# Layer 1's down projection in four parts of seven block products each

## The chip, the core and the metric

The kernel runs on one core of a Trainium2 chip. The metric is the device time of one execution in microseconds (us); smaller is better. Five engines run their own queues of instructions in order: TensorE (PE, with weight loads listed apart as PEld), VectorE (DVE), ScalarE (ACT), GpSimd (POOL) and SyncE (SP). Here SP issues the loads of the weights from HBM, and POOL issues transfers that add one buffer onto another on their way. An instruction waits for others by semaphores.

## What is computed

A trunk of two layers on 512 tokens of width 1024, all in float32. Each layer has a mixer and then a gated feed-forward network (FFN) of width 2816, both with a residual. The part that matters is the FFN:

```python
def gated_conv_ffn(x, w_gate, w_up, conv_w, conv_b, w_down):
    g = jnp.einsum('bsd,df->bsf', x, w_gate)
    g = causal_dwconv3(g, conv_w) + conv_b
    up = jnp.einsum('bsd,df->bsf', x, w_up)
    return jnp.einsum('bsf,fd->bsd', jax.nn.silu(g) * up, w_down)
```

After layer 1 follow the residual, `h = h + gated_conv_ffn(...)`, and a final RMSNorm.

## The kernel before

**Numbers in two parts.** The matmuls run in a format (F32R) shorter than float32. Each operand is therefore split: `hi` is the value rounded by an ACT copy, `lo` is the rest, by a DVE subtraction. A product is three matmuls: hi hi, hi lo, lo hi (`mm3`, L132). Weights come through `fetch` (L108: a load on SP's queue into a buffer with tag `raw`, of which there are 4, 512 KB each) and then `parts` (L125: ACT copy, DVE subtraction) or `summed` (L114). `summed` makes `lo` without DVE: ACT writes the negative of the rounded value (L120), POOL issues a transfer that adds the raw value onto it (L121), and ACT copies the `hi` (L122). Split weights lie in buffers with tags `whi` and `wlo`, 6 each.

**The FFN in tiles.** The 2816 hidden columns are 22 tiles of 128. They are made in pairs by `hidden(f)`. Pairs 0 and 2 are plain (`direct`). Pairs 4, 6, 10, 14 and 18 go through `both`, pairs 8, 12, 16 and 20 through `seven`: these form the gate and up projections (`seven`: the up projection only) as seven products of half blocks in place of eight, a scheme in which sums of weight blocks and of input blocks are multiplied and the products added up in the end. Their matmuls have 256 columns, 12 to a product. The names `s12`, `s34`, `s23`, `s14`, `a11` are such weight blocks; `kept` holds up results, `rows` is the padded gate tile for the convolution. Then `conv` (L502: an ACT copy and two DVE steps at L507), `silu` (L511, ACT), the product of gate and up (DVE), and `act` (L516), which splits the 128 x 512 result into `a_hi` and `a_lo`.

**The down projection of layer 1** is interleaved with that. `PARTS` says which pairs are made before which range of tiles is projected:

```python
PARTS = (((0, 2), 0, 2), ((4,), 2, 6), ((6, 8), 6, 10), ((10, 12), 10, 14),
         ((14, 16), 14, 18), ((18, 20), 18, 22))
```

In `ffn1` (L957) each part fetches its down weights one tile at a time (128 rows x 1024, `dn`), and `group8` (L1038) runs 8 PSUM banks: 4 blocks of 128 tokens by 2 halves of 512 output columns. For each bank it goes over the part's tiles, with the activations as the stationary operand and 512 columns of weights as the moving one: 3 matmuls for each tile and bank, 96 for four tiles. When a bank is complete, DVE adds it onto `y` (L1010), which began as the transposed residual. In the last part (tiles 18 to 21) the final norm follows.

**Order.** The kernel's text gives the dependencies, and a scheduler fixes ahead of time the order of instructions on each engine and the buffer that each tile gets. In that order the first matmuls of a part's down projection are those of its two older tiles, for several banks, and those of the two younger ones come in later. PSUM has 7 banks for matmul results and one for other uses.

Of the kernel before, what the change touches and what calls it, by code (L numbers as in the profile page):

```python
# [30 lines left out]
def tile_trunk(ctx: ExitStack, tc: tile.TileContext, x, norm_mix, norm_ffn, final_norm,  # L31
# [3 lines left out]
    nc = tc.nc  # L35
    x = x[0]
# [4 lines left out]
    tp = ctx.enter_context(tc.tile_pool(name="tp", bufs=2))  # L41
# [3 lines left out]
    def mm_bank(name):  # L45
        return ps_mm.tile([P, 512], F32, tag="mm", name=name)
# [61 lines left out]
    def fetch(src, a, b, name):  # L108
        raw = wp.tile([P, a, b], F32, tag="raw", bufs=4, name=f"raw_{name}")
        nc.sync.dma_start(raw, src)  # L110
        return raw, a, b, name

    def weights(src, a, b, name):
        return parts(*fetch(src, a, b, name))  # L114

    def summed(raw, a, b, name):

        hi = wp.tile([P, a, b], F32R, tag="whi", bufs=6, name=f"whi_{name}")
        lo = wp.tile([P, a, b], F32R, tag="wlo", bufs=6, name=f"wlo_{name}")
        nc.scalar.activation(lo, raw, AF.Copy, scale=-1.0)  # L120
        nc.gpsimd.dma_start(lo, raw, accum_op=ALU.add)  # L121
        nc.scalar.activation(hi, raw, AF.Copy)  # L122
        return hi, lo

    def parts(raw, a, b, name):  # L125
        hi = wp.tile([P, a, b], F32R, tag="whi", bufs=6, name=f"whi_{name}")
        lo = wp.tile([P, a, b], F32R, tag="wlo", bufs=6, name=f"wlo_{name}")
        nc.scalar.activation(hi, raw, AF.Copy)  # L128
        nc.vector.tensor_tensor(lo, raw, hi.bitcast(F32), ALU.subtract)  # L129
        return hi, lo  # L130
# [113 lines left out]
    def split(pool, src, name, scale=1.0, tag="a", bufs=None):  # L244
        hi = pool.tile([P, S], F32R, tag=f"{tag}hi", bufs=bufs, name=f"{name}_hi")
        lo = pool.tile([P, S], F32R, tag=f"{tag}lo", bufs=bufs, name=f"{name}_lo")
        nc.scalar.activation(hi, src, AF.Copy, scale=scale)  # L247
        if isinstance(scale, float):
            nc.vector.tensor_tensor(lo, src, hi.bitcast(F32), ALU.subtract)  # L249
        else:  # L250
            nc.vector.scalar_tensor_tensor(lo, src, scale, hi.bitcast(F32),
                                           op0=ALU.mult, op1=ALU.subtract)
        return hi, lo
# [223 lines left out]
    HALF = S // 2  # L477
# [10 lines left out]
    class Ffn:  # L488
# [5 lines left out]

        def __init__(self, layer, prm, norm, ap, sums):
            self.layer, self.prm, self.ap, self.acts = layer, prm, ap, {}
            self.norm, self.sums = norm, sums
            self.t23, self.t41 = {}, {}  # L500

        def conv(self, t, ft):  # L502
            ap, prm, n = self.ap, self.prm, f"{self.layer}_{ft}"
            c = ap.tile([P, S], F32, tag="c", bufs=2, name=f"c{n}")
            nc.scalar.activation(c, t[:, 0:S], AF.Copy, scale=prm("cf", ft))
            for i in (1, 2):
                nc.vector.scalar_tensor_tensor(c, t[:, i : S + i], prm("cf", i * NF + ft), c,  # L507
                                               op0=ALU.mult, op1=ALU.add)
            return c

        def silu(self, c, ft):  # L511
            s = self.ap.tile([P, S], F32, tag="s", bufs=3, name=f"s{self.layer}_{ft}")
            nc.scalar.activation(s, c, AF.Silu, bias=self.prm("bf", ft))  # L513
            return s

        def act(self, ft, s):  # L516
            self.acts[ft] = split(self.ap, s, f"a{self.layer}_{ft}", tag="a", bufs=4)

        def pair_weights(self, f, order, by_dma=""):

# [439 lines left out]
    def ffn1(norm):  # L960
        with tc.tile_pool(name="f1", bufs=1) as ap:
            def sums(kp):
                return [cp.tile([P, 2, HALF], F32R, tag=f"h{k}", name=f"t23_{k}")
                        for k in (kp, kp + NP)]

            ffn = Ffn(1, prm1, norm, ap, sums)
            acts = ffn.acts
            y = [ap.tile([P, D], F32, name=f"y{t}") for t in range(NT)]
            ssf = ap.tile([P, NT, PAD], F32, name="ssf")[:, :, :2]

            def turn_residual(t, half):
                ps = mm_bank(f"hT{t}_{half}")
                for i in range(4):
                    nc.tensor.transpose(ps[:, i * P : (i + 1) * P],
                                        h[half * 4 + i][:, t * P : (t + 1) * P], ident)
                nc.scalar.copy(y[t][:, half * 512 : (half + 1) * 512], ps)

            def before(i, j):
                if i < 2:
                    turn_residual(j, i)  # L980

            for groups, a, b in PARTS:
                for f in groups:
                    ffn.hidden(f, before=before)
                last = b == NF
                if last:
                    fin = wp.tile([P, D], F32, tag="raw", bufs=4, name="fin")
                    nc.scalar.dma_start(
                        fin, final_norm.rearrange("(o d) -> o d", o=1).to_broadcast([P, D]))
                    root = small[:, 2:3]  # L990
                    nc.scalar.activation(root, eps, AF.Sqrt)
                ch = {}
                for ft in range(a, b):
                    ch[ft] = weights(w_ffn_down[1][ft * P : (ft + 1) * P, :]
                                     .rearrange("(k p) c -> p k c", p=P), 1, D, f"dn1_{ft}")

                def lhs(ft, j):
                    ts_ = slice((j // 2) * P, (j // 2 + 1) * P)
                    return acts[ft][0][:, ts_], acts[ft][1][:, ts_]

                def rhs(ft, j):
                    c = slice((j % 2) * 512, (j % 2 + 1) * 512)
                    return ch[ft][0][:, 0, c], ch[ft][1][:, 0, c]

                yf = {}

                def done(j, ps):
                    t, half = j // 2, j % 2
                    dst = y[t][:, half * 512 : (half + 1) * 512]
                    nc.vector.tensor_tensor(dst, ps, dst, ALU.add)  # L1010
                    if not last:
                        return
                    sq = tp.tile([P, S], F32, tag="sq", name=f"sqf{j}")
                    ss = ssf[:, t, half : half + 1]
                    nc.scalar.activation(sq, dst, AF.Square, accum_out=ss)
                    yf[half] = ap.tile([P, S], F32, tag="s", bufs=3, name=f"yf{j}")
                    nc.vector.tensor_tensor(yf[half], dst, fin[:, half * 512 : (half + 1) * 512],
                                            ALU.mult)
                    if half == 0:
                        nc.vector.tensor_scalar(ss, ss, 1.0 / D, EPS, op0=ALU.mult, op1=ALU.add)  # L1020
                        return
                    ms = ssf[:, t, 0:1]
                    nc.vector.scalar_tensor_tensor(ms, ss, 1.0 / D, ms, op0=ALU.mult, op1=ALU.add)
                    r = tp.tile([P, LINE], F32, tag="rc", name=f"rc_fin{t}")[:, :1]
                    newton(ms, 1, f"fin{t}", r)
                    nc.vector.tensor_scalar(ms, ms, 1.5, None, op0=ALU.add)
                    for c in range(2):
                        cs = slice(c * 512, (c + 1) * 512)
# [18 lines left out]
    n = mixer0()  # L1047
    n = ffn0(n)
    n = mixer1(n)
    ffn1(n)  # L1050


# [28 lines left out]
```

## Time and profile before

| | us |
|---|---|
| median of 3 runs | 1006.06 |
| fastest, slowest run | 1005.46, 1007.25 |
| span of the profiled execution | 1004.4 |

The profile is of one execution. Its span reaches from its first to its last instruction; no other time is listed for that execution. Times inside it are counted from the span's start. Layer 1's FFN is the last third, about 640 to 1004 us. A row of a timeline gives the start, the duration, the engine, the line and operation, what is written and what is read, and in brackets the idle time before it and what ended it. A row of the stage table gives, for a stretch, the busy time of each engine with the number of instructions. The chain of waits follows the work that ended last back through what released it.

### The profile page before, as it was taken

What the parts mean: (1) busy time and instruction counts of PE and PEld (TensorE: products, weight loads), DVE (VectorE), ACT (ScalarE), POOL (GpSimd) and SP (SyncE); (2) the same over time, 40 slices, a digit from 0 to 9 for tenths busy, and PEclk for the clock granted to TensorE, in tenths of its full rate; (3) what the DMA queues carried; (4) which work ended last, traced back from release to release, by engine and by line L of the source; (5) the groups of instructions that cost most, each with busy time, mean ns of one, the idle gap of its engine ahead of it and who ended that gap; (6) DMA issues with size and microseconds to landing.
All of it is one profiled execution on the core that took longest, in us unless ns stands there. A gap on an engine that the chain in (4) does not pass through costs nothing.

```text
span 1004.4 us, 14019 instructions
## 1 busy us (share of the span) xinstructions
PE 992.1 (99%) x5547; PEld 865.9 (86%) x5547; DVE 666.0 (66%) x993; ACT 499.9 (50%) x735; POOL 94.1 (9%) x109
## 2 busy tenths in 40 slices
PE   8999999999999999999999999999999999999997
PEld 6888888898989989899878888888989898898985
DVE  5977457968584775847833645389675857658567
ACT  6523345754553635537645434675535365353553
POOL 3032030200000000000300001212000000000000
PEclk9999999999999999999999999999999999999999
DMA  7532234554445444454433123435545345353432
GB/s 236 178 105 84 85 90 122 117 155 114 118 142 131 128 110 119 138 137 127 127 125 104 63 85 105 101 88 123 150 100 153 105 127 147 94 152 112 127 85 84
DMA packets 80749, 120.30 MB, mean 120 GB/s; under 512 B 4164, under 2 KB 53548, under 8 KB 80684
## 3 DMA queue, kind: packets, MB, share of 16 engines
q1 hardware_dynamic: 73580, 98.96, 30.9%
q0 software_dynamic: 5760, 18.88, 10.7%
q10 hardware_dynamic: 1344, 1.58, 0.5%
q8 instruction: 43, 0.70, 0.3%
q14 instruction: 22, 0.18, 0.1%
HBM read 98.42 MB, written 2.10 MB: 100 GB/s over the span
## 4 chain that ended last, share of the span: by engine, by line
PE 95%; DMA 2%; DVE 2%; ACT 1%; SPq 0%; issue 0%; POOL 0%; DVEq 0%; ACTq 0%; POOLq 0%
PE dn L133 4%; PE dn L135 4%; PE dn L134 4%; PE d L133 4%; PE d L134 4%; PE d L135 4%; PE gu L133 3%; PE g L133 3%; PE g L134 3%; PE gu L134 3%; PE gu L135 3%; PE g L135 3%; PE u L135 1%; PE oo L133 1%; PE oo L135 1%; PE u L134 1%
## 5 line engine op out<-in xcount | busy, mean ns | idle before, releaser
L507 DVE SCALAR_TENSOR_TENSOR c<-rows,prm,c 128x512 f32<-128x512 f32 x88 | 68.9, 792 | 0.3
L134 PE MATMUL d<-a_lo,whi_d 128*128 128x512 f32 x176 | 68.6, 390 | 0.0
L135 PE MATMUL d<-a_hi,wlo_d 128*128 128x512 f32 x176 | 68.5, 389 | 0.0
L133 PE MATMUL dn<-whi_dn,a_hi 128*128 128x512 f32 x176 | 68.4, 390 | 0.0
L134 PE MATMUL dn<-wlo_dn,a_hi 128*128 128x512 f32 x176 | 68.4, 390 | 0.0
L135 PE MATMUL dn<-whi_dn,a_lo 128*128 128x512 f32 x176 | 67.6, 390 | 0.0
L133 PE MATMUL d<-a_hi,whi_d 128*128 128x512 f32 x176 | 67.1, 390 | 0.0
L1010 DVE TENSOR_TENSOR y<-dn,y 128x512 f32<-128x512 f32 x48 | 32.3, 688 | 30.9 <-PE dn L135 30.7
L133 PE MATMUL g<-hgh,whi_g 128*128 128x512 f32 x128 | 50.0, 391 | 0.0
L134 PE MATMUL g<-hgl,whi_g 128*128 128x512 f32 x128 | 50.0, 391 | 0.0
L135 PE MATMUL g<-hgh,wlo_g 128*128 128x512 f32 x128 | 49.8, 389 | 0.0
L129 DVE TENSOR_TENSOR wlo_dn<-raw_dn,whi_dn 128x1024 fp32r<-128x1024 f32 x22 | 26.8, 1222 | 30.7 <-ACT whi_dn L128 30.7
L129 DVE TENSOR_TENSOR wlo_d<-raw_d,whi_d 128x1024 fp32r<-128x1024 f32 x22 | 26.8, 1221 | 30.2 <-ACT whi_d L128 30.2
L129 DVE TENSOR_TENSOR wlo_u<-raw_u,whi_u 128x1024 fp32r<-128x1024 f32 x16 | 19.6, 1223 | 34.2 <-ACT whi_u L128 34.1
L120 ACT ACTIVATE wlo_g<-raw_g 128x1024 fp32r<-128x1024 f32 x14 | 14.7, 1050 | 51.6 <-PE dn L134 51.6
L292 DVE TENSOR_TENSOR h<-d,h 128x512 f32<-128x512 f32 x48 | 32.4, 686 | 11.6 <-PE d L135 11.1
L513 ACT ACTIVATE s<-c,prm 128x512 f32<-128x512 f32 x44 | 31.6, 718 | 16.7 <-DVE c L507 16.6
L135 PEld LDWEIGHTS dn<-whi_dn,a_lo 128*128 128x128 f32 x176 | 33.0, 188 | 7.4 <-DVE a_lo L249 0.2
L134 PEld LDWEIGHTS d<-a_lo,whi_d 128*128 128x128 f32 x176 | 33.1, 188 | 7.1 <-DVE a_lo L249 0.2
L133 PEld LDWEIGHTS dn<-whi_dn,a_hi 128*128 128x128 f32 x176 | 33.1, 188 | 7.0 <-ACT a_hi L247 0.2
L133 PEld LDWEIGHTS d<-a_hi,whi_d 128*128 128x128 f32 x176 | 32.9, 188 | 7.0
L135 PEld LDWEIGHTS d<-a_hi,wlo_d 128*128 128x128 f32 x176 | 33.0, 188 | 6.8
(972 smaller groups left out, 3196.0 us busy)
## 6 DMA issues: line engine op xcount, KB each, us to landing
raw_g<-in_w_ffn_gate_dram SPq DMA_DIRECT2D x36, 512.0 KB, 4.5
raw_u<-in_w_ffn_up_dram SPq DMA_DIRECT2D x36, 512.0 KB, 3.8
raw_d<-in_w_ffn_down_dram SPq DMA_DIRECT2D x22, 512.0 KB, 3.6
raw_dn<-in_w_ffn_down_dram SPq DMA_DIRECT2D x22, 512.0 KB, 4.4
wlo_u<-raw_u POOLq DMA_DIRECT2D x18, 512.0 KB, 5.2
wlo_g<-raw_g POOLq DMA_DIRECT2D x14, 512.0 KB, 4.5
raw_oe<-in_w_out_even_dram SPq DMA_DIRECT2D x8, 512.0 KB, 3.5
raw_g<-in_w_ffn_gate_dram SPq DMA_DIRECT2D x16, 256.0 KB, 2.9
```

The costliest lines, as they stand in the source:

```text
L120: nc.scalar.activation(lo, raw, AF.Copy, scale=-1.0)
L129: nc.vector.tensor_tensor(lo, raw, hi.bitcast(F32), ALU.subtract)
L133: nc.tensor.matmul(ps, lhs[0], rhs[0], start=start, stop=False)
L134: nc.tensor.matmul(ps, lhs[0], rhs[1], start=False, stop=False)
L135: nc.tensor.matmul(ps, lhs[1], rhs[0], start=False, stop=stop)
L292: nc.vector.tensor_tensor(h[k], ps, h[k], ALU.add)
L507: nc.vector.scalar_tensor_tensor(c, t[:, i : S + i], prm("cf", i * NF + ft), c, op0=ALU.mult, op1=ALU.add)
L513: nc.scalar.activation(s, c, AF.Silu, bias=self.prm("bf", ft))
L1010: nc.vector.tensor_tensor(dst, ps, dst, ALU.add)
```

## The change

For the four parts with tiles 2 to 17, the down projection of four tiles is done by a new function, `down(a)`. It takes the activations as a 2 x 2 block matrix (two halves of 256 tokens by two pairs of tiles) and the weights as one (two pairs of tiles by two halves of 512 output columns), and forms seven products of sums of blocks. A product has 2 token blocks x 2 tiles x 3 matmuls of 512 columns, 84 for the seven. Their results share three pairs of banks: products 1, 6, 7 and 4 add up in pair `a`, 5 and 3 in pair `e`, and 2 has pair `b`. After each product the pair's current content is added onto `y`, so the next product onto the same pair has to wait for that addition, and there are 14 additions for 8.

The weights of a part come as four blocks of 256 rows x 512 columns (`b11`, `b21`, `b12`, `b22`). Four weight sums (t1 to t4) are formed by DVE, three of them in place in the raw buffers, and all four are split by `summed`; b11, b21 and b22 by `parts`. The activations of tiles 2 to 17 are not split by `act` any more. The rows of two tiles stay in one float32 buffer (`rows`), and `down` forms four sums and splits seven blocks of 128 x 2 x 256. To make room, the convolution's tile `c` takes buffers that other temporaries share, and the pair of `silu` rows is one tile in both layers.

The core of the diff:

```diff
         def conv(self, t, ft):
-            c = ap.tile([P, S], F32, tag="c", bufs=2, name=f"c{n}")
+            c = tp.tile([P, S], F32, tag="sq", name=f"c{n}")
...
         def silu(self, c, ft):
-            s = self.ap.tile([P, S], F32, tag="s", bufs=3, name=f"s{self.layer}_{ft}")
+            f = ft - ft % 2
+            if f not in self.rows:
+                self.rows[f] = self.ap.tile([P, 2, S], F32, tag="s", bufs=3,
+                                            name=f"s{self.layer}_{f}")
+            s = self.rows[f][:, ft % 2, :]
...
         def act(self, ft, s):
-            self.acts[ft] = split(self.ap, s, f"a{self.layer}_{ft}", tag="a", bufs=4)
+            if ft not in self.kept:
+                self.acts[ft] = split(self.ap, s, f"a{self.layer}_{ft}", tag="a",
+                                      bufs=4 if self.layer == 0 else 3)
...
-            ffn = Ffn(1, prm1, norm, ap, sums)
+            ffn = Ffn(1, prm1, norm, ap, sums, range(2, 18))
...
+            def down(a):
+                g1, g2 = ffn.rows[a], ffn.rows[a + 2]
+                name = f"dn{a}"
+
+                def part(src, n, by_dma=False):
+                    hi = ap.tile([P, 2, HALF], F32R, tag="ahi", bufs=3, name=f"hi{n}_{a}")
+                    lo = ap.tile([P, 2, HALF], F32R, tag="alo", bufs=3, name=f"lo{n}_{a}")
+                    nc.scalar.activation(hi, src, AF.Copy)
+                    nc.vector.tensor_tensor(lo, src, hi.bitcast(F32), ALU.subtract)
+                    return hi, lo
...
+                a11, a21 = g1[:, :, :HALF], g1[:, :, HALF:]
+                a12, a22 = g2[:, :, :HALF], g2[:, :, HALF:]
+                b11, b21, b12, b22 = block(0, 0), block(1, 0), block(0, 1), block(1, 1)
+                mov, stat = {}, {}
+                mov[1] = parts(*b11)
+                stat[1] = part(a11, 1)
+                mov[2] = parts(*b21)
+                t1, t4, t3 = b11[0], b21[0], b12[0]
+                minus(t1, b12[0], b11[0])
+                t2 = ap.tile([P, 2, 512], F32, tag="sum", bufs=3, name=f"t2_{a}")
+                minus(t2, b22[0], t1)
+                mov[6] = summed(t2, 2, 512, f"{name}_t2")
+                mov[5] = summed(t1, 2, 512, f"{name}_t1")
+                minus(t3, b22[0], b12[0])
+                mov[7] = summed(t3, 2, 512, f"{name}_t3")
+                minus(t4, b21[0], t2)
+                mov[3] = parts(*b22)
+                mov[4] = summed(t4, 2, 512, f"{name}_t4")
+
+                s1, s2 = (tp.tile([P, 2, HALF], F32, tag="rstd", name=f"as{i}_{a}")
+                          for i in range(2))
+                nc.vector.tensor_tensor(s1, a21, a22, ALU.add)
+                stat[2] = part(a12, 2)
+                minus(s2, s1, a11)
+                stat[6] = part(s2, 6)
+                stat[5] = part(s1, 5)
+                minus(s1, a11, a21)
+                stat[7] = part(s1, 7)
+                minus(s2, a12, s2)
+                stat[3] = part(s2, 3)
+                stat[4] = part(a22, 4)
+
+                chain = {1: "a", 2: "b", 6: "a", 5: "e", 7: "a", 3: "e", 4: "a"}
+                onto = {1: (0, 0), 2: (0, 0), 6: (0, 1), 5: (1, 1), 7: (1, 1), 3: (0, 1),
+                        4: (1, 0)}
+                banks = {}
+                for product in (1, 2, 6, 5, 7, 3, 4):
+                    (hi, lo), (whi, wlo) = stat[product], mov[product]
+                    half, c = onto[product]
+                    for i in range(2):
...
+                        for k in range(2):
+                            for l, r, end in ((hi, whi, False), (hi, wlo, False),
+                                              (lo, whi, k == 1)):
+                                nc.tensor.matmul(ps, l[:, k, ts_], r[:, k, :], start=first,
+                                                 stop=end, skip_group_check=True)
+                                first = False
+                        dst = y[2 * half + i][:, c * 512 : (c + 1) * 512]
+                        nc.vector.tensor_tensor(dst, ps, dst, ALU.add)
...
+                if a in (2, 6, 10, 14):
+                    down(a)
+                    continue
```

Here `block(r, c)` fetches the rows of tile pair `r` and the columns of half `c`, `minus(dst, x, y)` is a DVE subtraction, and `mm_bank` gives a PSUM bank. In the text below hi2 and lo2 are the two parts of the activation block of product 2, and so on.

More of the change, by code (lines that the diff above doesn't have):

```diff
@@ L488, in tile_trunk, with __init__ @@
     class Ffn:
-        def __init__(self, layer, prm, norm, ap, sums):
+        def __init__(self, layer, prm, norm, ap, sums, kept=()):
             self.layer, self.prm, self.ap, self.acts = layer, prm, ap, {}
@@ L500, in __init__ @@
             self.t23, self.t41 = {}, {}
+            self.rows, self.kept = {}, kept
         def conv(self, t, ft):
             ap, prm, n = self.ap, self.prm, f"{self.layer}_{ft}"
-            c = ap.tile([P, S], F32, tag="c", bufs=2, name=f"c{n}")
+            c = tp.tile([P, S], F32, tag="sq", name=f"c{n}")
             nc.scalar.activation(c, t[:, 0:S], AF.Copy, scale=prm("cf", ft))
@@ L964, in sums @@
                         for k in (kp, kp + NP)]
-            ffn = Ffn(1, prm1, norm, ap, sums)
+            ffn = Ffn(1, prm1, norm, ap, sums, range(2, 18))
             acts = ffn.acts
-            y = [ap.tile([P, D], F32, name=f"y{t}") for t in range(NT)]
+            y_all = ap.tile([P, NT, D], F32, name="y")
+            y = [y_all[:, t, :] for t in range(NT)]
             ssf = ap.tile([P, NT, PAD], F32, name="ssf")[:, :, :2]
@@ L980, in before, with block, minus @@
                     turn_residual(j, i)
+            def down(a):
[7 more added lines that the diff above has]
+                    return hi, lo
+                def block(r, c):
+                    rows = slice((a + 2 * r) * P, (a + 2 * r + 2) * P)
+                    return fetch(w_ffn_down[1][rows, c * 512 : (c + 1) * 512]
+                                 .rearrange("(k p) c -> p k c", p=P), 2, 512, f"{name}_{r}{c}")
+                def minus(dst, x, y_):
+                    nc.vector.tensor_tensor(dst, x, y_, ALU.subtract)
+                a11, a21 = g1[:, :, :HALF], g1[:, :, HALF:]
[36 more added lines that the diff above has]
+                    for i in range(2):
+                        at = chain[product], i
+                        first = at not in banks
+                        if first:
+                            banks[at] = mm_bank(f"{name}{at[0]}{i}")
+                        ps = banks[at]
+                        ts_ = slice(i * P, (i + 1) * P)
+                        for k in range(2):
[6 more added lines that the diff above has]
+                        nc.vector.tensor_tensor(dst, ps, dst, ALU.add)
@@ L1015, in done @@
                     nc.scalar.activation(sq, dst, AF.Square, accum_out=ss)
-                    yf[half] = ap.tile([P, S], F32, tag="s", bufs=3, name=f"yf{j}")
+                    if half == 0:
+                        yf["pair"] = ap.tile([P, 2, S], F32, tag="s", bufs=3, name=f"yf{j}")
+                    yf[half] = yf["pair"][:, half, :]
                     nc.vector.tensor_tensor(yf[half], dst, fin[:, half * 512 : (half + 1) * 512],
```

## The prediction

> **What bounds the kernel now.** I read the page first (span, busy time, the shares of the chain that ended last), then the busy time by stage, then the timelines of the engines around one down projection of layer 1.
>
> ```profile
> span 1004.4 us, 14019 instructions
> PE 992.1 (99%) x5547; PEld 865.9 (86%) x5547; DVE 666.0 (66%) x993; ACT 499.9 (50%) x735; POOL 94.1 (9%) x109
> ...
> PE 95%; DMA 2%; DVE 2%; ACT 1%; SPq 0%; issue 0%; POOL 0%; DVEq 0%; ACTq 0%; POOLq 0%
> ```
>
> TensorE carries 95% of the chain. One part of the layer (here tiles 6 to 9) has three stages; the columns are length, then busy time of PE, PEld, DVE, ACT and POOL, clock, DMA share, GB/s.
>
> ```profile
> 744.40:764.70 20.30, 20.30 (x170) 20.18 (x170) 13.42 (x19) 12.35 (x19) 0.86 (x1) 1.00 0.58 156
> 764.70:785.70 21.00, 21.00 (x134) 19.09 (x133) 14.52 (x22) 13.86 (x22) 0.85 (x1) 1.00 0.55 151
> 785.70:807.50 21.80, 21.80 (x99) 17.98 (x98) 14.12 (x23) 4.53 (x6) 0.85 (x1) 1.00 0.26 73
> ```
>
> First row: hidden tiles 6 and 7 (`both`), second: 8 and 9 (`seven`), third: the down projection. TensorE never pauses; the others have room on average. How fast it goes is read from starts, since busy times overlap (48 down matmuls, then the first of the next stage):
>
> ```profile
> 691.37 0.39 PE L133 MATMUL dn<-whi_dn,a_hi 128*128 128x512 f32 x1
> ...
> 702.03 0.39 PE L135 MATMUL dn<-whi_dn,a_lo 128*128 128x512 f32 x1
> 702.25 0.28 PE L624 MATMUL g_4a<-hgh,whi_a 128*128 128x256 f32 x1
> 702.37 0.28 PE L624 MATMUL g_4a<-hgl,whi_a 128*128 128x256 f32 x1
> ```
>
> (702.25 - 691.37)/48 = 0.2267 us for each 512-column matmul, and 0.12 for a 256-column one; the 0.39 is a latency.
>
> **What the change removes.** A part has 4 tiles x 8 banks x 3 = 96 matmuls; the seven products have 12 each, 84. So 12 x 0.2267 = **2.72 us less per part, 10.9 in four**: the down stage would last 19.04 instead of 21.8.
>
> **What it adds.** Durations as steps between back-to-back starts:
>
> ```profile
> 745.15 1.23 DVE L634 TENSOR_TENSOR wlo_s34g<-s34g,whi_s34g 128x1024 fp32r<-128x1024 f32 x1
> 746.30 1.22 DVE L634 TENSOR_TENSOR wlo_s12u<-s12u,whi_s12u 128x1024 fp32r<-128x1024 f32 x1
> 747.43 0.69 DVE L730 TENSOR_TENSOR s<-raw_u,raw_u 128x512 f32<-128x512 f32 x1
> 748.03 0.69 DVE L732 TENSOR_TENSOR s<-raw_u 128x512 f32<-128x512 f32 x1
> ...
> 783.09 0.75 DVE L507 SCALAR_TENSOR_TENSOR c<-rows,prm,c 128x512 f32<-128x512 f32 x1
> 783.75 0.42 DVE L769 TENSOR_TENSOR kept<-u_8b,kept 128x256 f32<-128x256 f32 x1
> 784.08 1.22 DVE L129 TENSOR_TENSOR wlo_dn<-raw_dn,whi_dn 128x1024 fp32r<-128x1024 f32 x1
> ```
> ```profile
> 743.13 1.04 ACT L122 ACTIVATE whi_g<-raw_g 128x1024 fp32r<-128x1024 f32 x1
> 744.08 1.04 ACT L633 ACTIVATE whi_s34g<-s34g 128x1024 fp32r<-128x1024 f32 x1
> ...
> 784.50 0.62 ACT L633 ACTIVATE whi_a<-raw_g 128x512 fp32r<-128x512 f32 x1
> 785.02 0.62 ACT L633 ACTIVATE whi_a<-raw_u 128x512 fp32r<-128x512 f32 x1
> ```
>
> DVE steps: 1.14 for 1024 elements, 0.60 for 512, 0.66 for a convolution tap, 0.33 for 256. ACT: 0.95 for 1024, 0.52 for 512. Per part DVE gains 6 additions into y (14 for 8; 3.6), 4 sums of weights less one split (3.4), 4 sums of activations (2.4) and 3 more splits (1.8): 11.2. Its three stages hold 13.42 + 14.52 + 14.12 = 42.1, so 53.3 of at best 60.4: 88%. ACT gains 7 instructions of 0.95 and 3 of 0.52: 8.2 on 30.7. Neither exceeds TensorE's time; what counts is which of them comes last at the points where TensorE needs it. POOL's queue gets four accumulating transfers of 512 KB per part, between the one of tile 8's up weights and those of the next tiles.
>
> Two edits I cost at nothing. The convolution tile moves to a shared pair of buffers and the silu rows become pairs: the changed kernel's order of instructions in layer 0 is the same on every engine, so nothing there is moved past anything. The balance of loads on SP's queue is equal (four of 512 KB for four).
>
> **Wait one: the second product.** The rows of the transfer chain before the down stage:
>
> ```profile
> 768.45 1.05 ACT L120 ACTIVATE wlo_u<-raw_u 128x1024 fp32r<-128x1024 f32 x1
> 769.79 0.85 POOL L121 DMA_DIRECT2D wlo_u<-raw_u  x1 [20.67 <-ACT wlo_u L120]
> 775.18 0.38 SPq L110 DMA_DIRECT2D raw_g<-in_w_ffn_gate_dram  x1
> ```
> ```profile
> 784.28 1.44 PE u_8e L624 x12
> ```
> ```profile
> DMA to landing us min/median/max: 5.3/6.6/7.0
> DMA to landing us min/median/max: 3.5/4.5/5.5
> ```
>
> (Timelines of ACT, POOL and SP; the chain; the landing times of the accumulating wlo_u transfers and of the raw_dn loads.) Call the down stage's start T0: 784.28 + 1.44 = 785.7. In before, the wlo_u accumulate was issued at 769.79 and SP's next load, which waits for its buffer, began at 775.18: landed 5.3 us after issue, at T0 - 10.5. In the changed kernel's allocation the fourth weight block (b22) takes this very buffer. ACT has one 0.5 us copy less ahead, so its load starts at T0 - 11.0 and lands 3.5 later, at **T0 - 7.5**. DVE's queue is in order, and t2 = b22 - t1 stands in it ahead of the rest of tile 8 and 9's gating. From there: t2, t3, the split of b21 and t4 (4 x 1.14) to T0 - 2.9; four convolution taps (2.6), two additions, two gate products and the last addition (5 x 0.33), the last product, s1, one addition into y, s2 (4 x 0.60), the split of b22 (1.14), and the low part of a12 (0.60): T0 + 5.5 without any wait. ACT, with eight of its added 0.95 us copies between the convolution's first taps and a12's high part, makes DVE wait about 0.8 more: **low part at T0 + 6.4, high part at T0 + 5.1**. TensorE has 2.72 us of product 1, then four matmuls with the high part, so it wants the low part at T0 + 3.63. It waits 6.4 - 3.6 = **2.8 us**. Bounds: 1.9 (no ACT wait, T0 + 5.5) and 3.8 (a load of 4.5).
>
> In before this lateness was covered: the last low part ended near T0 + 4.1,
>
> ```profile
> 789.22 0.69 DVE L249 TENSOR_TENSOR a_lo<-s,a_hi 128x512 fp32r<-128x512 f32 x1
> ```
>
> and TensorE had eight banks of the two older tiles to do first. Now the cover is one product.
>
> **Wait two: product 7.** Queued behind the two lines of unit 10's a11 on ACT are hi7, hi3 and hi4. The second of those lines reads raw_u_10, whose buffer is that of b12, free when t3's accumulate has landed. ACT finishes t3's negative copy at about T0 + 2.6, POOL issues at 2.9; landing 5.3 to 7.0, I take 5.7 (three transfers follow one another): 8.6. Load 3.5 to 4.5, I take 3.9: 12.5; a11 and hi7 on ACT: 13.6. On DVE, lo7 and lo3 stand ahead of the y addition that frees product 7's bank: 13.7 + 3 x 0.60 = 15.5. TensorE is there at 10.88 + 2.8 = 13.7: it waits **1.8 us**. Since product 7 starts when that addition is done, the two waits together have its ends: 15.5 - 10.88 = 4.6; with the fastest transfers (5.3 and 3.5) the addition ends at 14.7, 3.8 together; with 7.0 and 5.5 at 18.4, 7.5.
>
> So the down stage lasts 19.04 + 2.8 + 1.8 = 23.6 against 21.8.
>
> **Wait three: the next hidden stage.** From T0 + 13.7 DVE has no pause: 23 instructions of 0.60 and 3 of 1.14 stand up to the low part of s12u, ready at about T0 + 31.4 where TensorE, with what the order puts ahead, is at 30.8: 0.6. ACT makes the copies of unit 10's second up half behind s12u's; its accumulate is issued at T0 + 32.3 and lands 5.3 later, 37.6, where TensorE is at 36.2: 1.4. Together **2.0**; ends 0.5 (half the DVE backlog) and 3.7 (landing 7.0).
>
> **Sum** per part: -2.72 + 2.8 + 1.8 + 2.0 = +3.9; four parts +15.6. The first part follows a `both` unit, whose gating ends later still (its silus stand after T0); I give it the same. The profiled execution has 1004.4 us of span; no time of its own is listed, and the median of the runs, 1006.06, is 1.7 above, which I carry over. 1006.1 + 15.6 = **1021.7**. With the lower ends (3.8 and 0.5: +1.6 per part) 1012.5, with the upper ones (7.5 and 3.7: +8.5) 1040; four parts do not all have the slowest transfers, so the case's own range is 1012 to 1032.
>
> **Rivals.**
> 1. *TensorE's count decides* (not slower): the static order's neighbours are later than my walk has them, so the waits vanish. The place is b22's buffer: were its load landed by T0 - 10.3 instead of T0 - 7.5, lo2 would come in time, and hi7 with it. Time: 1006.1 - 10.9 = **995**, to 1002 with a wait of under 2 per part. For it: DVE at 88%, ACT near 65%. Against: SP's start at 775.18. Chance 0.15.
> 2. *Wait one only*: waits two and three hang on accumulates that land 5.3 or later. If they landed 3.5 after issue, like the fastest plain load above, t3 would be in at 6.4, b12's buffer refilled at 10.3, hi7 done at 11.4 and the y addition at 13.3, before TensorE's 13.7; DVE's backlog would end 2.2 earlier and the last accumulate land at 35.8, before 36.2. Then -2.72 + 2.8: **1006.4**, 1002 to 1010. It decides from a landing of about 3.9. Against: the rows, 5.3 to 7.0. Chance 0.14. [...]
> 3. *The clock falls in a gap.* These rows are a gap in before, and its end:
>
> ```profile
> 507.48 0.66 PE L851 MATMUL wst<-ident,ws 128*128 128x128 f32 x4 [1.55 <-POOL ws L844]
> 504.00:508.00 4.00, 2.45 (x14) 1.00 0.76 265
> 996.67 0.39 PE L135 MATMUL dn<-whi_dn,a_lo 128*128 128x512 f32 x1
> 1001.00:1002.00 1.00, 0.00 (x0) 0.94 0.76 283
> 1002.00:1003.00 1.00, 0.00 (x0) 0.50 0.65 242
> ```
>
> A pause of 1.55 left the clock at 1.00; after the last matmul (996.67 + 0.39) it went to 0.50 near 1001.9, 4.8 us on. Wait one is between. If every wait one passes that point, one product at half clock costs 2.72 more per part: 1021.7 + 10.9 = **1033**. Chance 0.08. [...]
>
> **Numbers.** Forecast 0.63 (1021.7), rivals 0.15, 0.14, 0.08. A measurement of this kernel tells about 0.2% from no change, 2 us: faster 0.15 + a sixth of rival 2 = 0.17; same 0.07; slower 0.76. The range must hold 8 in 10: 1002 to 1032 leaves out rival 1 and most of rival 3.
>
> **What would show it.** In the changed profile: down matmuls per part 84 at 0.227; TensorE waiting at product 2 for DVE's lo of a12 by 2 to 4 us; SP's b22 load waiting for the accumulate of wlo_u; the y addition before product 7 late behind lo7; TensorE waiting in the next `both` for wlo_u. If TensorE shows no idle time in a part, rival 1 is right; if only at product 2, rival 2; a granted clock under 1.00 within layer 1, rival 3. The prediction falls if the fourth block's load starts well before T0 - 11.

## The result, and the profile after

The changed kernel takes **1049.65 us** (median of 4 runs, 1045.23 to 1051.71), the kernel before 1005.76 on the same chip: a ratio of 1.0429, 95% interval 1.0402 to 1.0456. The forecast was 1021.7 with a range to 1032: the sign is right, the time is 28 us beyond it. The profiled execution has a span of 1049.2 us. Its page (span, busy time, chain by engine):

```profile
span 1049.2 us, 14117 instructions
PE 999.5 (95%) x5499; PEld 866.1 (83%) x5499; DVE 707.9 (67%) x1057; ACT 533.6 (51%) x775; POOL 107.6 (10%) x125
...
PE 72%; DMA 11%; DVE 9%; ACT 4%; issue 3%; POOL 1%; SPq 0%; DVEq 0%; ACTq 0%; POOLq 0%
```

The 48 matmuls fewer are there (5499 for 5547), and TensorE's share of the chain has fallen from 95% to 72%. The three stages of the part of tiles 6 to 9 (columns as in the prediction):

```profile
751.20:774.40 23.20, 20.97 (x170) 20.34 (x169) 16.59 (x25) 12.61 (x20) 1.70 (x2) 1.00 0.60 160
774.40:798.20 23.80, 21.47 (x134) 19.15 (x134) 16.04 (x22) 13.74 (x21) 2.31 (x3) 1.00 0.33 84
798.20:825.10 26.90, 21.48 (x86) 16.66 (x85) 20.43 (x34) 11.97 (x17) 1.99 (x3) 0.94 0.61 142
```

All three are longer: 23.2 for 20.3, 23.8 for 21.0, 26.9 for 21.8. What TensorE waited for in layer 1 (waiter, what it waited for, total, times, longest):

```profile
PE dn2b L1058 <- ACT hi L997: 4.8, 1, 4.8
PE dn14a L1058 <- DVE y L1062: 4.4, 1, 4.4
PE dn6a L1058 <- DVE y L1062: 4.0, 1, 4.0
PE dn10a L1058 <- DVE y L1062: 3.4, 1, 3.4
PE u_14b L631 <- DMA wlo_u<-raw_u: 2.6, 1, 2.6
...
PE u_8e L631 <- DVE kept L776: 1.8, 1, 1.8
...
PE dn6b L1058 <- ACT hi L997: 1.3, 1, 1.3
```

`dn..b` is product 2, `dn..a` waiting for y is product 7, `u_14b` is in the next `both`, and `u_8e` in `seven`, where I had no wait. The chain through that part, from the accumulate that frees b22's buffer to product 7 (start, length, what):

```profile
779.08 6.67 DMA wlo_u<-raw_u
...
785.82 3.49 DMA raw_dn<-in_w_ffn_down_dram
...
797.63 0.83 POOL wlo_dn_t L121
...
800.21 5.32 DMA wlo_dn_t<-raw_dn
...
805.61 6.42 DMA raw_u<-in_w_ffn_up_dram
...
812.58 0.62 ACT hi L997
...
813.84 0.69 DVE lo L998
814.52 0.61 DVE y L1062
...
815.27 4.59 PE dn6a L1058 x12
```

These are the links that the prediction named: t3's accumulate, the load behind it, hi7 behind that load on ACT, lo7 ahead of the y addition. But the load took 6.4 us (6.3 and 6.9 in the next two parts), not 3.9. And product 7 took 4.42 us from its first matmul's start to that of the next product (4.59 to the end of its last), where twelve matmuls at full pace take 2.72. Up to 818.7 its matmuls start 0.43 us apart, from 819.0 on 0.23. The clock column says why (PE's busy time, granted clock, DMA share, GB/s):

```profile
812.00:815.40 3.40, 0.13 (x1) 1.00 0.67 218
815.40:818.80 3.40, 3.40 (x9) 0.51 0.02 5
866.70:870.10 3.40, 1.63 (x13) 0.99 0.50 96
870.10:873.50 3.40, 3.40 (x11) 0.50 1.03 193
907.60:911.00 3.40, 1.82 (x16) 1.00 0.58 116
911.00:914.40 3.40, 2.33 (x19) 1.00 0.76 234
```

After the windows that were 96% and 52% idle (812.0, 866.7) the next one runs at half clock (815.4, 870.1); after one 46% idle (907.6) it doesn't (911.0). From 700 to 1005 us TensorE has 35.2 us of recorded idle time. In seven windows at half clock it is busy for 23.1 us. By the clock column (0.51 and 0.50 in the two rows at 815.4 and 870.1) half of that is lost, so half clock costs another 11.5, an estimate.

One loss lies outside the parts. From the last matmul's end (1038.5) to the end are 10.7 us; in before they were 7.4. I call this stretch the tail. ACT's longest wait in the last stage:

```profile
ACT a_hi L247 <- PE dn L134: 9.1, 1, 9.1
```

The change leaves three buffers for split activations in layer 1 instead of four (the `act` line of the diff). The last part needs four, so its fourth tile is split 9.1 us late, all eight banks finish late, and the output work piles up behind the last matmul.

The account closes. From the start of tile 4's stage to that of tile 20's: 292.5 us (702.88 to 995.40) for 251.75 in before, +40.8; the tail +3.3; 0.6 elsewhere: 44.7 of the 44.8 between the spans.

### The profile page after: what moved, and what is told of

Its sections match the earlier page's. It is cut to its first block, busy times and chain, and to the rows that moved or that the text cites. A ratio compares the mean times of both kernels' runs of the same rounds, so it can differ in the third digit from the quotient of the medians.

```text
span 1049.2 us, 14117 instructions
## 1 busy us (share of the span) xinstructions
PE 999.5 (95%) x5499; PEld 866.1 (83%) x5499; DVE 707.9 (67%) x1057; ACT 533.6 (51%) x775; POOL 107.6 (10%) x125
## 4 chain that ended last, share of the span: by engine, by line
PE 72%; DMA 11%; DVE 9%; ACT 4%; issue 3%; POOL 1%; SPq 0%; DVEq 0%; ACTq 0%; POOLq 0%
DMA wlo_u<-raw_u 4%; PE d L134 3%; PE d L133 3%; PE d L135 3%; PE gu L133 3%; PE gu L135 3%; PE gu L134 3%; DMA raw_u<-in_w_ffn_up_dram 2%; PE g L134 2%; PE g L133 2%; PE g L135 2%; DVE y L1062 2%; DMA wlo_dn_t<-raw_dn 2%; DMA raw_g<-in_w_ffn_gate_dram 2%; PE u L135 1%
## 5 line engine op out<-in xcount | busy, mean ns | idle before, releaser
L121 POOL DMA_DIRECT2D wlo_u<-raw_u x18 | 15.4, 858 | 253.0 <-ACT wlo_u L120 186.3
L292 DVE TENSOR_TENSOR h<-d,h 128x512 f32<-128x512 f32 x48 | 32.4, 685 | 12.0 <-PE d L135 11.7
L518 ACT ACTIVATE s<-c,prm 128x512 f32<-128x512 f32 x44 | 31.5, 718 | 15.4 <-DVE c L508 15.3
L129 DVE TENSOR_TENSOR wlo_g<-raw_g,whi_g 128x1024 fp32r<-128x1024 f32 x20 | 24.4, 1219 | 16.3 <-ACT whi_g L128 16.3
L189 POOL TENSOR_TENSOR ssq_f<-ssq_f,sq_f 128x512 f32<-128x512 f32 x12 | 16.3, 1359 | 179.9 <-ACT sq_f L188 145.0
L121 POOL DMA_DIRECT2D wlo_g<-raw_g x14 | 12.2, 873 | 218.2 <-ACT wlo_g L120 95.4
L640 ACT ACTIVATE whi_s12u<-s12u 128x1024 fp32r<-128x1024 f32 x10 | 10.6, 1062 | 46.8 <-PE d L134 32.2
L175 ACT ACTIVATE hgh<-h,prm 128x512 fp32r<-128x512 f32 x24 | 17.3, 720 | 32.0 <-DVE h L292 32.0
L128 ACT ACTIVATE whi_g<-raw_g 128x1024 fp32r<-128x1024 f32 x20 | 21.0, 1051 | 23.6 <-DMA raw_g<-in_w_ffn_gate_dram 9.9
L640 ACT ACTIVATE whi_s12g<-s12g 128x1024 fp32r<-128x1024 f32 x10 | 10.6, 1062 | 42.6 <-DVE s12g L661 42.6
```

The source lines that it names most:

```text
L175: nc.scalar.activation(hg[k][0], h[k], AF.Copy, scale=g)
L292: nc.vector.tensor_tensor(h[k], ps, h[k], ALU.add)
L640: nc.scalar.activation(hi, src, AF.Copy)
```

## Theory and rivals

**A.** The waits are made by a chain of buffers (an accumulate that lands late holds a raw buffer, the next load waits for it) read by in-order queues on ACT and DVE, plus the clock that falls behind a long pause (to half at 815.4, behind one of 4.0 us). **B.** DVE, with 11 us more per part (its three stages above hold 53.1 us), is the bound; the waits only show its backlog. Within A it is open which link decides: the buffer that b22 takes, t3's accumulate, the order of ACT's queue, or all of them.

## The experiments

All edits are to the changed kernel, except in the control at the end. Times are medians; each set ran beside the kernel before, which took 1004.4 to 1005.4.

**b22 loaded third**

```diff
-b11, b21, b12, b22 = block(0, 0), block(1, 0), block(0, 1), block(1, 1)
+b11, b12, b22, b21 = block(0, 0), block(0, 1), block(1, 1), block(1, 0)
```

> Only the order of the four weight loads of a part is changed: b11, b12, b22, b21. The buffer freed by the accumulate of the second up half (landing 6 to 7 us after issue) now goes to b21, not to b22, so that t2 and t3 on DVE need not wait for it, only the split of b21 and t4. Theory A (a chain of buffers: accumulate, load, in-order DVE and ACT queues, and the clock that falls after a long pause): two sums of 1.14 us are done while b21 is awaited, everything behind them comes 2.3 us earlier, and the pause before product 7 gets shorter than 4 us, so that half of its clock loss goes too: 2.3 to 5 us per part, 1036 us (1028 to 1042). Theory B (DVE, with 11.2 us more per part, is the bound): its work is the same, 1049 us, within 3.

Measured 1052.65 us: no gain, a miss for A as I had stated it, and near B's 1049. In the part of tiles 6 to 9 the wait in `seven` has gone, but the one at product 7 has grown:

```profile
PE dn6a L1058 <- DVE y L1062: 6.6, 1, 6.6
PE dn6b L1058 <- ACT hi L997: 1.4, 1, 1.4
```

The links ahead of product 7 took longer here: from the issue of t3's accumulate to ACT's copy of the up weights loaded behind it are 14.4 us (793.75 to 808.17), in the changed kernel 11.8 (800.21 to 812.05).

**t3 split by DVE**

```diff
-mov[7] = summed(t3, 2, 512, f"{name}_t3")
+mov[7] = parts(t3, 2, 512, f"{name}_t3")
```

> t3 is split by ACT and DVE in place of ACT and an accumulating transfer, so that the buffer of b12 comes free without a landing of 5 us. DVE gets 1.14 us more per part. Theory A: the load of unit 10's up weights starts 5 us earlier, the wait of 3.4 to 4.4 us before product 7 goes, and with it the clock loss behind it (1.4 to 2.2 us); the 1.14 us of DVE comes back at product 2: about 4 us less per part, 1034 us (1028 to 1042). Theory B: slower by the added DVE time, 4 x 1.14, 1054 us.

Measured 1032.0 us (1029.0 to 1041.3, all below the changed kernel's fastest). With *more* DVE work it is 18 us faster: B falls. The scheduler also put the first three matmuls of the next stage ahead of product 7 here, so the edit is not quite pure.

**No accumulates in `down`**

```diff
 def summed(raw, a, b, name, add=True):
...
-        nc.gpsimd.dma_start(lo, raw, accum_op=ALU.add)
+        if add:
+            nc.gpsimd.dma_start(lo, raw, accum_op=ALU.add)
```

with `add=False` for the four weight sums. This kernel leaves out the transfers that complete their low parts.

> Leaves out the four accumulating transfers of each down part (the low parts of the four weight sums are then only the negative copies); DVE's and ACT's work is unchanged. Theory A: the waits before product 7 (0.9 + 4.0 + 3.4 + 4.4 = 12.7 us over the four parts), the clock losses behind them (some 5) and part of the waits for wlo_u in the next stage (6.4) go: 1028 us (1022 to 1034). The waits at product 2 and inside the stage before it stay. Theory B: DVE's work is unchanged, 1049 us, within 3.

Measured 1029.0 us: the waits before product 7 are gone, those at product 2 and in `seven` are about as before, and those for `wlo_u` in the next `both` of the three later parts are 2.4 to 2.7 us (1.1 to 2.6 in the changed kernel). The transfers also stretch the loads beside them. Up loads in layer 1 (median us from issue to landing, last column), first the changed kernel, then without the accumulates:

```profile
raw_u<-in_w_ffn_up_dram SPq DMA_DIRECT2D x16, 512.0 KB, 4.9
```
```profile
raw_u<-in_w_ffn_up_dram SPq DMA_DIRECT2D x16, 512.0 KB, 3.7
```

**Fillers in the pauses**

```diff
+if product in (2, 7):
+    (fh, _), (fw, _) = (stat[1], mov[1]) if product == 2 else (stat[6], mov[6])
+    fill = aux_bank(f"fill{product}_{a}")
+    for i in range(6 if product == 2 else 12):
+        nc.tensor.matmul(fill, fh[:, 0, :P], fw[:, 0, :], start=True, stop=True, ...)
```

> Adds matmuls that nothing reads, into the spare bank: six (1.36 us) ahead of product 2 and twelve (2.72 us) ahead of product 7, where TensorE waits anyway. They shorten its pauses and not its waits. Theory A with the clock as a term: the waits stay, the clock holds 1.00 behind product 7's pause (4 us less 2.7) and mostly at product 2; minus 1.4 to 2.5 us per part, plus up to 1 us where a wait is shorter than its fillers: 1043 us (1038 to 1048). If the pauses do not lower the clock, or the half-speed rows have another cause: 1050 to 1054 us.

Measured 1034.49 us: **16.3 us of useless matmuls make the kernel 15.2 us faster.** The half-clock loss falls from 11.5 to 1.7 us and the idle time from 35.2 to 12.5. The sum of the three (+16.3 - 9.8 - 22.7) is -16.2. So about 9.8 us of the gain are the clock's. The other 6.4 (22.7 - 16.3) are waits that shrank by more than their fillers, in the neighbouring stages too. That beat the range, and I did not separate it.

**ACT's order**

```diff
 def halves(self, hi, lo, src, pin=False):
-    nc.scalar.activation(hi, src, AF.Copy)
+    copy = nc.scalar.activation(hi, src, AF.Copy)
+    if pin:
+        inorder(copy)
...
-self.halves(w[0][:, i], w[1][:, i], raws[key, 0][0][:, :, :P])
+self.halves(w[0][:, i], w[1][:, i], raws[key, 0][0][:, :, :P],
+            layer == 1 and f > 4)
```

(in `both`, for the first copies of units 6, 10, 14 and 18. `inorder` makes the scheduler keep an instruction in the order of the kernel's text; I call that copy pinned.)

> The first copy of the next unit's weights on ACT is pinned behind the copies hi7, hi3 and hi4 of the down stage, so that these no longer stand behind a copy that waits for a load; nothing else is changed. Theory A1 (the wait before product 7 is made by the order of ACT's queue in front of the late load): the waits of 0.9 + 4.0 + 3.4 + 4.4 us before product 7 go, and the clock losses behind them (about 5): some of it comes back in the next stage, 1036 us (1030 to 1042). Theory A2 (the late load itself is what counts, the order only says where TensorE meets it): the wait moves into the next stage, 1045 us or more. Theory B (DVE's work is the bound): 1049 us.

Measured 1033.37 us, as A1 has it. ACT's timeline: hi7 (804.71), hi3 and hi4 now stand ahead of the copies that wait for the load.

```profile
804.71 0.63 ACT L1000 ACTIVATE hi<-as 128x512 fp32r<-128x512 f32 x1 [2.12 <-DVE as L1010]
805.72 0.63 ACT L1000 ACTIVATE hi<-as 128x512 fp32r<-128x512 f32 x1 [0.38 <-PE dn6a L1061]
808.44 0.63 ACT L1000 ACTIVATE hi<-s 128x512 fp32r<-128x512 f32 x1 [2.09 <-PE dn6e L1061]
808.98 0.61 ACT L640 ACTIVATE whi_a<-raw_g 128x512 fp32r<-128x512 f32 x1
809.50 0.62 ACT L640 ACTIVATE whi_a<-raw_u 128x512 fp32r<-128x512 f32 x1
```

TensorE no longer waits at product 7 in the parts of tiles 6, 10 and 14, with its own order of products around the down stage as in the changed kernel; the load may land late, since its data are wanted a stage later. In the first part that wait is 2.5 us (0.9 in the changed kernel), and the next stage's waits for `wlo_u` are 2.3 to 2.7 us, so a part of what A2 expected is there too.

**Up half split in `seven`**

```diff
-hi, lo = summed(*raws["u", 1])
+hi, lo = (parts if layer else summed)(*raws["u", 1])
```

> In the seven-product stage of layer 1 (tiles 8, 12, 16 and 20) the second up half is split by ACT and DVE in place of ACT and an accumulating transfer, so that the buffer which b22's load takes comes free without a landing of 6 to 7 us. DVE gets 1.14 us more per part. Theory A: b22 lands some 5 us earlier, DVE is not held by t2, the waits inside that stage (1.8 + 0.5 per part) and at product 2 (0.7 to 1.3) go in the parts of tiles 6, 10 and 14, and product 7's wait gets shorter by 1 to 4: 1032 us (1026 to 1040). The part of tiles 2 to 5 stays as it is (4.8 us at product 2). Theory B: slower by DVE's time, 1054 us.

Measured 1049.52 us, unchanged: a miss for A again, and not the 4 us slower that B wants. In the three later parts the waits in `seven` are gone and those at product 2 down to 1.0 us, but product 7's are 5.9, 5.7 and 6.0 us. The chain of the part of tiles 6 to 9, whose down stage begins at 793.21:

```profile
794.41 6.18 DMA wlo_dn_t<-raw_dn
800.66 7.78 DMA raw_u<-in_w_ffn_up_dram
```

t3's accumulate starts 1.2 us after the down stage's first matmul (2.0 in the changed kernel), because on ACT the copy for it stands behind tile 9's silu, not behind b22. The transfers, now closer together, took 14.0 us in place of 11.7. So product 7 begins 18.5 us into the stage instead of 17.1: what was gained ahead of it was spent there, and the half-clock loss rose to 15.4.

**Both**

The two edits above together.

> The edits of the two kernels before together: the pinned copy on ACT, and the second up half of layer 1's seven-product stages split by ACT and DVE. Theory A: the two waits have separate releases, so most of both gains adds up: 1022 us (1012 to 1030). Theory A2: no better than the better of the two. Theory B: 1054 us.

Measured 1024.70 us: the up split, worth nothing alone, is worth 8.7 us once product 7 does not wait.

**Both splits, no pin**

The t3 split and the up split together.

> Two accumulating transfers per part are replaced by splits on ACT and DVE: that of the second up half in layer 1's seven-product stages and that of t3. DVE gets 2.28 us more per part. Theory A: both buffers come free early: the gain of the t3 split (18 us measured) and most of that of the up split: 1018 us (1010 to 1028). Theory B, with DVE near 55.6 of 60.4 us per part: 1059 us; a mixed case, in which DVE's backlog becomes the bound, would stay at 1030 to 1035.

Measured 1036.34 us: A's expectation failed, and it lies just above the range of the mixed case. The next stage's first matmuls come ahead of product 7 as in the t3 kernel, product 7 still waits 2.2 us in each of three parts, the next stage 2.1 us for an accumulate, and half clock costs 11.5 us. Why it is slower than the t3 split alone stays open.

**Next stage's up half split too**

```diff
-hi, lo = summed(*raws[key, 1])
+hi, lo = (parts if layer and key == "u" else summed)(*raws[key, 1])
```

> The kernel with the pinned ACT copy and the split up half of the seven-product stages (1024.7 us), and the second up half of layer 1's two-unit stages is split by ACT and DVE too, so that the product of the next stage that waited 1.4 to 2.2 us for an accumulating transfer has none to wait for. DVE gets 1.14 us more per part. Theory A: these waits (5.6 us in three parts) and the clock loss behind them go: 1017 us (1011 to 1022). Theory B (DVE's backlog sets the low part's time as much as the transfer did): 1024 to 1030 us.

Measured 1013.96 us: wait three is gone.

**Three parts**

```diff
-ffn = Ffn(1, prm1, norm, ap, sums, range(2, 18))
+ffn = Ffn(1, prm1, norm, ap, sums, range(6, 18))
...
-if a in (2, 6, 10, 14):
+if a in (6, 10, 14):
```

and four buffers for the split activations, those of `act` and those of `down` (tags `ahi` and `alo`). Three kernels have this edit: one with the pin and the up split, one with all edits, and one with nothing else.

> The kernel with the pinned ACT copy and the split up half of the seven-product stages (1024.7 us), but tiles 2 to 5 are done as in the kernel before (their activations split, 96 matmuls), so that only three parts have seven products; the activation splits have four buffers in place of three. The part of tiles 2 to 5 has waits of 4.8 and 2.5 us and a half-clock window or two (some 4 us) in that kernel, for 2.72 us saved: 1016 us (1011 to 1020). If the wait only moves to the next part: 1022 to 1026.

> All edits together: three parts, the pinned ACT copy, and the second up half of both kinds of hidden stage of layer 1 split by ACT and DVE. Theory A: what stays are waits of about 1 us at product 2 in three parts, against 8.2 us saved: 1006 us (1000 to 1012). Theory B (DVE, now with 13.5 us more per part than before, is the bound): 1015 us or more.

> The changed kernel with only three parts in seven products (tiles 6 to 17) and four buffers for the activation splits; no other edit. By the table of waits the part of tiles 2 to 5 costs 4.8 + 0.9 us of waiting, some 3 of half clock and 2 in the next stage, less 2.72: 1041 us (1037 to 1044). If the four parts cost the same, 1038.7 (a quarter of 43.9 less).

Measured 1011.14, **1002.70** and 1043.11 us. The middle one is a quarter of a per cent faster than the kernel before: ratio 0.9973, 0.9963 to 0.9983. In these kernels the tail is 7.4 us, so part of the gain is the fourth buffer's. That was tested by itself:

> The changed kernel with four buffers in place of three for the split activations (tags of hi and lo in layer 1), nothing else. If the fourth tile of the last part waits for a buffer and so holds the last additions: the stretch behind the last matmul goes from 10.7 to 7.4 us and the time from 1049.7 to 1046.3 us (1044 to 1048), with the waits of the parts as they were. If the three-part form made it: 1049.7 us, tail 10.7.

> The four-part kernel with the pinned ACT copy and both up halves split (1014.0 us), with four buffers for the split activations. The tail goes from 10.7 to 7.4: 1010.6 us (1009 to 1012). Then the part of tiles 2 to 5 in seven products costs 1010.6 - 1002.7 = 8 us of its own. If the third buffer also made the wait of 4.8 us at that part's product 2: 1005 to 1007.

Measured 1046.12 and 1008.84 us, both with a tail of 7.4: having three buffers in place of four cost 3.3. ACT's wait of 9.1 us for `a_hi` is gone, so it is `act`'s buffer that counts, though the edit gives `down` a fourth one too. Product 2 of the first part still waits 4.8 us in both. Then the part of tiles 2 to 5 costs about 3.0 in the changed kernel (1046.12 to 1043.11, with ranges that overlap) and 6.1 in the mended one (1008.84 to 1002.70); in the changed one the waits at product 7 get longer without it (5.8, 5.4 and 5.0 us for 4.5, 4.6 and 4.8).

**Controls and the pin again**

The kernel before with both up halves split; the best kernel with b22 third; the best kernel without the pin.

> The kernel before, with only the second up halves of layer 1 split by ACT and DVE in place of ACT and an accumulating transfer (both kinds of hidden stage). TensorE has no wait there to lose, so if the three parts in seven products are what gains: 1005.2 us, within 1.5. If the split edits are what beat the kernel before: 1002 to 1003.

> The kernel with all edits (1002.7 us) with the order of the weight loads b11, b12, b22, b21. If the wait of 1.0 us at product 2 is b22's landing, which holds DVE: 2 to 3 us less in three parts, 1000 us. If it is DVE's and ACT's own work before the low part of a12: 1002 to 1003.

> The kernel with all edits (1002.7 us) without the pinned ACT copy. If the wait before product 7 is ACT's order in front of a load of 6 to 8 us and needs no other wait beside it: 5 to 6 us of pause in each of three parts, as in the kernel with the up half split, and 1.7 to 3.4 of half clock behind each: 1002.7 + 3 x 7 to 9 = 1024 to 1030 us. If it came from the delays ahead of it: 1003 to 1008.

Measured 1004.77 (ratio 0.9995, 0.9986 to 1.0003), 1002.43 and 1029.87 us. The split edits give the kernel before nothing, so the gain is the seven products' own. (The pin was not tried on the kernel before, where no wait of TensorE is recorded in these stages.) b22 third changes nothing there. And the order on ACT alone is worth 27 us, with every other wait at 1 us or less:

```profile
PE dn6a L1058 <- DVE y L1062: 7.8, 1, 7.8
PE dn14a L1058 <- DVE y L1062: 6.5, 1, 6.5
PE dn10a L1058 <- DVE y L1062: 6.5, 1, 6.5
```

In the best kernel the clock is 1.00 throughout the three parts, and its stages are (tiles 6 to 9):

```profile
743.50:763.60 20.10, 20.10 (x169) 20.10 (x168) 14.38 (x20) 11.38 (x18) 0.12 (x1) 1.00 0.47 131
763.60:784.60 21.00, 21.00 (x134) 19.09 (x133) 17.93 (x24) 13.33 (x21) 1.71 (x2) 1.00 0.23 67
784.60:805.20 20.60, 19.63 (x86) 15.64 (x85) 19.73 (x32) 11.19 (x15) 1.71 (x2) 1.00 0.80 189
```

From one down stage to the next are 62.35 us (784.62 to 846.97) where before had 63.15: 0.8 of the 2.72 is kept, and 0.9 in each of the next two parts, which makes nearly all of the gain (2.5 us by the medians). What is still lost is mostly product 2, 0.5 for ACT's hi and 0.5 for DVE's lo.

## Why the forecast was wrong

The mechanism was the one foretold: late accumulates, loads behind them, in-order queues. Three steps of the sum failed. Wait two was sized too small (4.15 us for 1.8), and two losses had no term in it: the wait inside `seven` (2.4) and the half clock (1.7). Against these, waits one and three were 1.45 us shorter than foretold. The four parts cost 12.0, 9.2, 10.1 and 9.4 us, 40.8 where 15.6 were forecast. That and the tail's 3.3 are nearly all of the 28 us; even the sum with the prediction's upper ends, 1040, lies below the measurement.

By the prediction's own steps, for the part of tiles 6 to 9 (72.35 us from one down stage to the next, for 63.15):

| step | foretold | measured |
|---|---|---|
| 12 matmuls less | -2.72 | -2.72 |
| wait one, product 2 | 2.8 | 1.75 |
| wait two, product 7 | 1.8 | 4.15 |
| half clock behind it | only in rival 3 | 1.7 |
| wait three, next `both` | 2.0 | 1.6 |
| wait inside `seven` | none | 2.4 |
| sum | +3.9 | +8.9; with 0.3 not assigned, +9.2 |

The waits are starts measured against TensorE's pace, so they are a little longer than the recorded idle times.

- **Wait one** had the right cause: b22's load follows the wlo_u accumulate (6.67 us, not 5.3), landing at 789.3. Its lateness showed first inside `seven`, where DVE, standing at t2, held the additions that free a bank TensorE needs. The prediction listed those additions behind t2 and priced only the low part of a12 at the end of the list; the consumer in the middle was not asked for. The two together are 4.15 us where 2.8 were foretold. In the first part, behind `both`, product 2 alone waited 4.8 us.
- **Wait two** is the step that failed most in size. t3's accumulate was issued 2.0 us into the stage (foretold 2.9) and took 5.3 (5.7), but the load behind it took 6.4, where I took 3.9 from loads of before, which has 13 accumulating transfers between 700 and 1000 us for 28 here. The four that the change adds to a part stretch it themselves: without them the median of the up loads falls from 4.9 to 3.7. The same error cut the range: I drew it in from 1040 to 1032 since "four parts do not all have the slowest transfers". They did: the load took 6.2, 6.4, 6.3 and 6.9 us in the four parts, each above the 5.5 of the slowest one that I had. The edit of ACT's order shows what this wait is worth with the half clock behind it: 16.3 us of the changed kernel, 27 in the best one.
- **The clock** was rival 3, with 0.08, tied to wait one at product 2. It fell once behind the first part's product 2 (730.1, for two windows), three times around product 7 (815.4, 887.1, 962.2) and twice around waits of 1.8 and 1.9 us in the neighbouring stages (870.1, 986.1): all but the first at pauses of 1.8 to 4.4 us, where my only witness was one of 4.8. With 11.5 us in the four parts it is a quarter of the loss, and the fillers show it.
- **Wait three** had the right place and size (0.8 to 2.6 for the accumulate).
- **The edits costed at nothing**: the convolution tile and the paired rows are not seen to cost anything (they are in the best kernel too; no run has them alone), but the diff's third edit of that kind, three activation buffers for four, was not looked at past layer 0. It costs 3.3 us at the very end.
- Rival 1 (TensorE's count decides) and rival 2 (only wait one) both fail: TensorE waited at every place named. Rival 2's landing of 3.5 us after issue does not hold for these transfers of 512 KB: 5.3 us is the median of `wlo_dn_t` from raw buffers, 6.2 of `wlo_u`.

What stays open: why the fillers shortened the waits of the neighbouring stages, and why the two splits without the pin do worse than the t3 split alone.

## What to carry to other kernels

On an engine's in-order queue, look for the first instruction that waits on a load and ask what stands behind it for the engine that is the bound: moving that back gave 16.3 us here with the up loads no faster (median 5.1 us for 4.9), against 20.7 for leaving out the accumulates. Price a transfer with the traffic that the change adds beside it (here a median of 4.9 us for the up loads, 3.7 without the four accumulates), and walk to every consumer of a late engine, not to the last. A wait removed ahead of a later wait that is anchored elsewhere gave nothing here until that one was gone (the up split: 1049.52 us for 1049.65 alone, 8.7 us less once ACT's order was changed), so such edits must be tried in pairs before one is dropped.

## What the runs showed of the hardware

**The clock's windows.** Read in steps of 0.1 us, the falls to half clock in six kernels (33 of them, six in the changed kernel: 730.1, 815.4, 870.1, 887.1, 962.2, 986.1) lie, within each kernel, on one grid of 3.41 us to within 0.05 (730.1 to 986.1 are 75 steps). A window at full clock that is 57% idle or more is followed in these runs by one at half clock, one of up to 45% is not; between, both happen. (One already at half clock can be followed by another with less: that from 730.1 was 18% idle.) So a pause of 1.8 us inside one window (867.0 to 868.8, the window 52% idle) cost 1.7 us of half speed, while another of 1.8 (794.9 to 796.7, the window 49% idle) and one of 2.6 us that a border cuts (909.4 to 912.0, the windows 47% and 31% idle) cost none.

**Accumulating transfers.** Of 512 KB within SBUF, issued by POOL, they took 4.5 to 8.5 us in the changed kernel's layer 1 (medians 4.5 for `wlo_g`, 6.2 for `wlo_u`). The load of up weights that runs beside the last accumulate of a part took 6.2 to 6.9 us there, and 7.8 in the kernel with the up half split; with the four accumulates left out, the same load took 3.5 and 4.4 in the two parts where its landing is recorded (the load after it also starts later there, so not all of this need be the accumulates'). The load at 785.82 in the chain above, with neither an accumulate nor another load beside it, took 3.5.
